# New keys appended to the page tiles of a decode attention, feature chunk innermost

## The chip, the cores and the metric

The kernel runs on one core of a Trainium2 chip. The metric is the device time of one execution in microseconds (us). TensorE (PE) multiplies matrices and writes to the accumulation banks (PSUM), VectorE (DVE), ScalarE (ACT) and GpSimd (POOL) work element by element, and SyncE (SP) issues most DMAs. Each engine works through its own instructions in order and waits on semaphores for the others.

## The reference

Two layers of a causal decoder, run on 256 prompt tokens and on 8 sample batches of 4 new tokens each. Four mixers (pooling, a 31-tap convolution module "conv", a short convolution, and a sparse attention) are gated and summed, and a SwiGLU follows. The change lies in the attention of the sample tokens. Each batch has 256 cached keys, in two pages of 128 rows that a page table names, and 4 new ones:

```
ki_all = concat([cache_kidx[row_ids], ki])            # indexer keys, cached then new
sc = index_scores(qi, ki_all, wi)                     # relu(q.k) weighted over 4 index heads
sc = where(arange(past + t) <= qpos, sc, -inf)        # a new token sees itself and earlier ones
vals, idx = top_k(sc, 65)
kg, vg = keys and values at idx                       # from the pages or from the new tokens
logits = einsum('nqhd,nqkhd->nqhk', q, kg) / 8
out = einsum('nqhk,nqkhd->nqhd', softmax(logits), vg) # 8 heads of 64 features
```

## The kernel before

All 288 tokens (256 prompt, 32 sample) lie along the free axis, features on the partitions. Weights come in 512 KB groups of eight 128x128 tiles. Each is split into a rounded part (`whi`, ACT, L245) and a remainder (`wlo`, DVE, L252) in float32r (fp32r), a format that PE takes in one pass; a float32 (fp32) matmul is split into two instructions. Every weight tile is used in three fp32r matmuls of 288 columns (L271 to L273; L293 to L297 where several outputs are interleaved).

**What sets the order.** The program is written out by a small planner. Weights are drawn by `W`; at each new group of eight tiles (24 matmuls) it counts one tick and calls `side`, which lets the side tasks go on: `index_prompt`, `index_sample`, `attn_prompt`, `attn_sample`, `sconv`, `pool`, and `conv` at low rank. A task is a generator: `yield n` makes it sleep n ticks, `yield d, a` charges the tick's budget of DVE and ACT time. The instructions that it issues stand in the engines' orders at that place. `finish` runs a task to its end. In `layer`, the projections come first, then gates (L1015) and branches (L1030) in turn; the attention and then conv tasks are finished before their branches. After the attention branch, layer 0 has 24 matmuls more (`pe_proj`) than layer 1; then the conv branch starts, interleaved with the first half of `w_o`.

**The conv task's end** in DVE and ACT order: centring (L677), squares (L680), a PE sum (L684), root (L686, ACT with a table load), reciprocal (L691), scaling (L696, L699), sigmoid (L702), product (L706), and in `parts` the rounded half (L633, ACT) and the remainder (L637, DVE), which the conv branch's matmuls take. `pe_load` splits another input there (L303 ACT, L304 DVE).

**The sample attention** runs in two halves `f` of four batches. A page tile `kv` (four buffers) holds both pages of one batch. Keys lie as `[128 features, page, chunk c of 4, 128 keys]`, so that one chunk of a page is 128 neighbouring values. One bank `a` of 128 rows (batch, head, token) takes the scores:
- L946: the bias of unselected keys, brought to the rows by a 0/1 matrix `selh`, in fp32;
- L949: for each chunk, all 32 new keys against all rows, into 32 columns behind the 256;
- L953: for each chunk and batch, that batch's page tile against its 32 rows (four column groups of the array, one per batch).

The bias masks the new keys of other batches too. Then DVE takes the row maximum (L958), ACT the exponential (L964), PE transposes the result (L972, L973), ACT copies it (L975, L976), PE multiplies with the values (L981 new, L984 pages). DVE scales by the reciprocal sum and blanks the other heads' columns (L988), four fp32 matmuls with a 0/1 matrix `sel16` gather the rows (L997), and ACT and DVE write rounded part and remainder (L1002, L1005) for the attention branch. In `index_sample` the cached indexer keys (L902) and the new ones (L904) are multiplied apart, into two banks.

Of the kernel before, what the change touches and what calls it, by code (L numbers as in the profile page):

```python
# [37 lines left out]
BIG = -1.0e30  # L38
# [12 lines left out]
def constants():  # L51
# [15 lines left out]
    ok = (b_[:, None] == b_[None, :]) & (t_[None, :] <= t_[:, None])  # L67
    vb = np.zeros((128, NS))
    vb[:NS] = np.where(ok, 0.0, NEG)
# [11 lines left out]
    c["selh"] = sh.reshape(128, 256)  # L81
    c["hmask"] = (h[:, None] == (np.arange(H))[None, :]) * 1.0
    c["sel16"] = ((j * TS + t)[:, None] == np.arange(16)[None, :]) * 1.0
# [10 lines left out]
    return [np.concatenate(p, 1).astype(np.float32) for p in parts], off  # L94


CONST, COFF = constants()
# [14 lines left out]
class Builder:  # L112
# [749 lines left out]
    def load_kidx(self):  # L862
        nc, l, d = self.nc, self.l, self.d
        self.kx = self.sb.tile([128, 4, 2, 128], F32, name="kv", tag="kv", bufs=4)
        rows = slice(PHYS * l, PHYS * (l + 1))
        for b in range(NB):
            for g in range(2):
                i = 2 * b + g
                if i not in self.page:
                    self.page[i] = nc.sync.value_load(self.pt[0:1, i:i + 1], min_val=0, max_val=PHYS - 1)  # L870
                nc.sync.dma_start(self.kx[64 * (b % 2):64 * (b % 2) + 64, b // 2, g],
                                  d["kidx"][rows][ds(self.page[2 * b + g], 1)].rearrange("a p k -> p (a k)"))
                yield 0, 0.01
            yield 1

    def load_pages(self, which, f):
        nc, l, d = self.nc, self.l, self.d
        rows = slice(PHYS * l, PHYS * (l + 1))
        out = []
        for b in range(4 * f, 4 * f + 4):  # L880
            t = self.sb.tile([128, 2, 4, 128], F32, name="kv", tag="kv", bufs=4)
            for g in range(2):
                nc.sync.dma_start(t[:, g].rearrange("p c k -> p (c k)"),
                                  d[which][rows][ds(self.page[2 * b + g], 1)].rearrange("a p k -> p (a k)"))
            out.append(t)
        yield 1
        return out

    def index_sample(self):
# [4 lines left out]
        for r in range(2):  # L894
            for h in range(4):
                nc.scalar.activation(self.qibd[64 * r:64 * r + 64, :, r, h],
                                     qv[64 * (h % 2):64 * (h % 2) + 64, h // 2, :, r], AF.Copy)
                yield 0, 0.22
        yield 1
        a, a2 = yield from self.get_ax(2)  # L900
        for p in range(4):
            nc.tensor.matmul(a[32 * p:32 * p + 32, :TP], self.qibd[:, p].rearrange("p r h t -> p (r h t)"),  # L902
                             self.kx[:, p].rearrange("p g k -> p (g k)"), start=True, stop=True)
        nc.tensor.matmul(a2[:, :NS], self.qibd.rearrange("p g r h t -> p (g r h t)"), self.ki[:, TP:],  # L904
                         start=True, stop=True)
        nc.tensor.matmul(a2[:, 64:64 + NS], self.c("hsel")[:4], self.wi[:, TP:], start=True, stop=True)
        rl = self.sb.tile([128, N], F32, name="rls", tag="rls", bufs=1)
        nc.scalar.activation(rl[:, :TP], a[:, :TP], AF.Relu, scale=0.0625)
        nc.scalar.activation(rl[:, TP:], a2[:, :NS], AF.Relu, scale=0.0625)
        yield 0, 0.6  # L910
        ws = self.sb.tile([128, NS], F32, name="ws", tag="ws", bufs=1)
        nc.vector.tensor_tensor(ws, a2[:, 64:64 + NS], self.c("delta"), op=OP.mult)
        self.free_ax(2)
# [3 lines left out]
        nc.tensor.matmul(a[:NS, :N], ws, rl, start=True, stop=True)  # L917
        sc = self.sb.tile([NS, N], F32, name="scs", tag="scs", bufs=1)
        nc.scalar.activation(sc[:, :TP], a[:NS, :TP], AF.Copy)
        nc.vector.tensor_tensor(sc[:, TP:], a[:NS, TP:N], self.c("vb")[:NS], op=OP.add)  # L920
        self.free_ax()
        yield 0.2, 0.3
        yield from self.topk(sc, NS, N, TOP_S)
        nc.vector.tensor_scalar(sc, sc, MARK, BIG, op0=OP.not_equal, op1=OP.mult)
        yield 0.3, 0
        self.sbias = sc

    def attn_sample(self):
# [12 lines left out]
        for f in range(2):  # L941
            if f:
                kt = yield from self.load_pages("ck", f)
                yield 1
            a = yield from self.get_ax()
            nc.tensor.matmul(a[:, :N], self.c("selh")[:NS, 128 * f:128 * (f + 1)], self.sbias,  # L946
                             start=True, stop=False)
            for c in range(4):
                nc.tensor.matmul(a[:, TP:N], self.qbd[:, c, 4 * f:4 * f + 4].rearrange("p b h t -> p (b h t)"),  # L949
                                 self.k[:, c, TP:], start=False, stop=False)  # L950
            for c in range(4):
                for j in range(4):
                    nc.tensor.matmul(a[32 * j:32 * j + 32, :TP],  # L953
# [4 lines left out]
            nc.vector.tensor_reduce(st[:, 0:1], a[:, :N], axis=AX.X, op=OP.max)  # L958
# [4 lines left out]
            p = self.sb.tile([128, N], F32, name="rls", tag="rls", bufs=1)  # L963
            nc.scalar.activation(p, a[:, :N], AF.Exp, scale=0.125, bias=st[:, 0:1], accum_out=st[:, 1:2])  # L964
# [8 lines left out]
            nc.tensor.transpose(a[:NS, 256:384], p[:, TP:], ident)  # L973
# [8 lines left out]
            for kc in range(2):  # L982
                for j in range(4):
                    nc.tensor.matmul(a[32 * j:32 * j + 32], pt[:, kc, 32 * j:32 * j + 32],  # L984
                                     vc[j][:, kc].rearrange("p c k -> p (c k)"),
                                     start=False, stop=kc == 1)
# [6 lines left out]
            yield 0.65, 0  # L993
# [7 lines left out]
            v = a[:, :64].rearrange("p (c t) -> p c t", c=4)  # L1001
            nc.scalar.activation(dp[0][:, :, w], v, AF.Copy)  # L1002
            yield 0, 0.25
            yield 1
            nc.vector.tensor_tensor(dp[1][:, :, w], v, dp[0][:, :, w].bitcast(F32), op=OP.subtract)  # L1005
            self.free_ax()
            yield 0.15, 0
# [192 lines left out]
    def run(self):  # L1200
# [56 lines left out]
class Pair:  # L1257
# [9 lines left out]
    "x": (128, KD, N), "w": (NGROUPS, 128, G * 128), "const0": CONST[0].shape, "const1": CONST[1].shape, "par": (L, 128, NPAR),  # L1267
# [35 lines left out]
def lay_out(inp, keys):  # L1303
# [9 lines left out]
    a["const0"], a["const1"] = CONST  # L1313
    par = np.zeros((L, 128, NPAR), f)
# [13 lines left out]
    for g in range(4):  # L1328
# [4 lines left out]
        inp["cache_k"].reshape(L * PHYS, PG, 4, 128).transpose(0, 3, 2, 1)).reshape(L * PHYS, 128, 512)  # L1333
# [40 lines left out]
```

## Time and profile before

| | us |
|---|---|
| median of three timed runs (lowest, highest) | 1090.82 (1090.24, 1092.0) |
| profiled execution, its own time | 1090.84 |
| its span, first to last instruction | 1089.1 |
| PE, DVE, ACT, POOL busy | 1066.8, 770.1, 560.7, 171.6 |

PE is busy nearly all the time, so its instructions set the time together with the few places at which it waits. A matmul's row in the timeline is longer than the step to the next one, since matmuls are pipelined: what one costs is read from start to start. Most of the sum is the 7344 weight matmuls; the sample attention is small beside them.

### The profile page before, as it was taken

The page shows a single profiled execution, that of the slowest core. Times are in us where ns is not written, and L with a number is a line of the kernel's source. Part 1 is how long each engine was busy: PE and PEld are TensorE (multiplying, and loading weights), DVE is VectorE, ACT ScalarE, POOL GpSimd, SP SyncE. Part 2 cuts the span into 40 slices and gives each one's busy share as a digit, 9 for nine tenths or more (in the row PEclk, how much of TensorE's full clock was granted, in tenths as well). Part 3 has the DMA queues.
Part 4 walks back from the last instruction along what each step waited for, and adds up shares of the span by engine and source line. Part 5 has one row for each costly group of instructions (what it writes and reads, how often), then busy time and mean ns, then how long its engine had stood idle before and what let it go on. Part 6 is the DMA issues. An engine that isn't in the chain of part 4 may idle for free.

```text
span 1089.1 us, 20628 instructions
## 1 busy us (share of the span) xinstructions
PE 1066.8 (98%) x8138; PEld 1030.1 (95%) x8138; DVE 770.1 (71%) x1302; ACT 560.7 (51%) x930; POOL 171.6 (16%) x175
## 2 busy tenths in 40 slices
PE   8999999999999999999999999999989999999996
PEld 7999989899999999999999999998989999999995
DVE  5896958579885565544789877776697856655456
ACT  4875445445564444433579564644535644444334
POOL 0730002004510000000527100030045000000004
PEclk9999999999999999999999999999989999999998
DMA  8576556644445455555445854565433654554541
GB/s 302 164 244 212 173 174 232 195 147 135 155 148 184 155 173 168 166 170 167 154 154 171 295 171 155 195 213 184 140 132 117 193 174 156 167 170 166 175 136 44
DMA packets 61299, 188.57 MB, mean 173 GB/s; under 512 B 7538, under 2 KB 11666, under 8 KB 61202
## 3 DMA queue, kind: packets, MB, share of 16 engines
q1 hardware_dynamic: 60210, 183.69, 51.7%
q0 software_dynamic: 992, 3.57, 0.9%
q8 instruction: 64, 1.05, 0.4%
q14 instruction: 33, 0.27, 0.1%
HBM read 182.48 MB, written 4.75 MB: 172 GB/s over the span
## 4 chain that ended last, share of the span: by engine, by line
PE 89%; DVE 5%; issue 2%; ACT 2%; POOL 2%; DMA 1%; SPq 0%; DVEq 0%; POOLq 0%
PE mm L271 24%; PE mm L272 24%; PE mm L273 23%; PE mm L295 2%; PE mm L297 2%; PE mm L293 2%; DVE wlo L252 2%; PE ax L272 1%; PE ax L273 1%; PE ax L271 1%; POOL b L317 1%; PE ax L295 1%; PE ax L297 1%; POOL b L348 1%; PE ax L953 1%
## 5 line engine op out<-in xcount | busy, mean ns | idle before, releaser
L252 DVE TENSOR_TENSOR wlo<-wraw,whi 128x1024 fp32r<-128x1024 f32 (+1 forms) x307 | 383.3, 1251 | 155.0 <-issue 83.8
L271 PE MATMUL mm<-xh,whi 128*128 128x288 f32 x1536 | 455.1, 296 | 0.0
L273 PE MATMUL mm<-xh,wlo 128*128 128x288 f32 x1536 | 453.1, 295 | 0.3 <-DVE wlo L252 0.3
L272 PE MATMUL mm<-xl,whi 128*128 128x288 f32 x1536 | 453.2, 295 | 0.0
L245 ACT ACTIVATE whi<-wraw 128x1024 fp32r<-128x1024 f32 (+1 forms) x307 | 322.6, 1052 | 148.1 <-PE mm L272 74.0
L271 PEld LDWEIGHTS mm<-xh,whi 128*128 128x128 f32 x1536 | 288.8, 188 | 8.1 <-issue 6.4
L273 PEld LDWEIGHTS mm<-xh,wlo 128*128 128x128 f32 x1536 | 288.6, 188 | 0.9 <-DVE wlo L252 0.9
L272 PEld LDWEIGHTS mm<-xl,whi 128*128 128x128 f32 x1536 | 288.8, 188 | 0.3
L271 PE MATMUL mm<-b,whi 128*128 128x288 f32 x576 | 171.0, 297 | 0.3 <-DVE s L1030 0.2
L272 PE MATMUL mm<-b,whi 128*128 128x288 f32 x576 | 169.9, 295 | 0.0
L273 PE MATMUL mm<-b,wlo 128*128 128x288 f32 x576 | 169.7, 295 | 0.0
L271 PEld LDWEIGHTS mm<-b,whi 128*128 128x128 f32 x576 | 108.3, 188 | 1.3 <-issue 0.4
L272 PEld LDWEIGHTS mm<-b,whi 128*128 128x128 f32 x576 | 108.3, 188 | 0.3
L273 PEld LDWEIGHTS mm<-b,wlo 128*128 128x128 f32 x576 | 108.2, 188 | 0.0
L1031 POOL TENSOR_TENSOR m<-m,s 128x288 f32<-128x288 f32 x32 | 35.3, 1129 | 274.6 <-DVE s L1030 274.6
L315 POOL TENSOR_TENSOR b<-xf 128x288 f32<-128x288 f32 x4 | 4.9, 1218 | 442.4 <-DVE xf L1176 433.5
L1149 ACT ACTIVATE b<-s 128x288 fp32r<-128x288 f32 x44 | 19.3, 446 | 92.4 <-DVE s L1144 92.4
L655 DVE SCALAR_TENSOR_TENSOR b<-b,prm 128x256 f32<-128x256 f32 x120 | 62.1, 569 | 0.0
L1144 DVE TENSOR_TENSOR s<-s,mm 128x288 f32<-128x288 f32 x40 | 18.0, 454 | 50.5 <-PE mm L273 50.5
L1015 ACT ACTIVATE g<-mm 128x288 f32<-128x288 f32 x32 | 13.2, 412 | 67.7 <-PE mm L273 67.7
L1015 ACT ACTIVATE xf<-mm 128x288 f32<-128x288 f32 x32 | 13.2, 411 | 51.1 <-PE mm L273 51.0
L1152 DVE TENSOR_TENSOR b<-s,b 128x288 fp32r<-128x288 f32 x44 | 19.8, 458 | 19.5 <-ACT b L1149 19.5
(254 smaller groups left out, 1243.7 us busy)
## 6 DMA issues: line engine op xcount, KB each, us to landing
wraw<-in_w_dram SPq DMA_DIRECT2D x305, 512.0 KB, 3.5
kv<-in_ck_dram SPq DMA_DIRECT2D x32, 256.0 KB, 5.0
kv<-in_cv_dram SPq DMA_DIRECT2D x32, 256.0 KB, 4.3
out_ko_dram<-b POOLq DMA_DIRECT2D x2, 576.0 KB, 4.7
out_vo_dram<-b POOLq DMA_DIRECT2D x2, 576.0 KB, 6.9
kv<-in_kidx_dram SPq DMA_DIRECT2D x32, 32.0 KB, 3.0
xf<-in_x_dram SPq DMA_DIRECT2D x3, 288.0 KB, 6.5
b<-in_p_dram SPq DMA_DIRECT2D x3, 288.0 KB, 4.0
```

Source lines behind the costliest of these rows:

```text
L245: nc.scalar.activation(t[:, c], self.raw[self.nhi][:, c], AF.Copy)
L252: nc.vector.tensor_tensor(t[:, c], raw[:, c], self.hi[self.nlo][:, c].bitcast(F32), op=OP.subtract)
L271: m(out, wh, rh, start=first, stop=False)
L272: m(out, wh, rl, start=False, stop=False)
L273: m(out, wl, rh, start=False, stop=last)
L293: m(o, wh, rh[:, k], start=k == 0, stop=False)
L295: m(o, wl, rh[:, k], start=False, stop=False)
L297: m(o, wh, rl[:, k], start=False, stop=k == nk - 1)
L655: nc.vector.scalar_tensor_tensor(o, e, wj, o, op0=OP.mult, op1=OP.add)
L1015: self.nc.scalar.activation(g, a, AF.Sigmoid)
L1031: nc.gpsimd.tensor_tensor(self.m[:, j], self.m[:, j], t, op=OP.add)
L1152: nc.vector.tensor_tensor(h[:, 1, i % 2], t, h[:, 0, i % 2].bitcast(F32), op=OP.subtract)
```

## The change

New keys become the last four columns of their batch's page tile. For that, the cached keys are laid out on the host with the four feature chunks innermost, a tile is `[128, 260 keys, 4]`, and ACT copies the new keys in (`add_new`). A chunk of a tile is then 260 values, each four values (16 bytes) behind the last. The scores have 260 columns in place of 288, the index scores too (there ACT copies the new indexer keys into the index tile, which stays contiguous). The bias constant becomes a power of two, the bias is written as fp32r, and `selh` is loaded apart and rounded once by POOL, so that L946's successor is one fp32r matmul. The probabilities of new keys are spread over the batches by a mask (`pn`, `own`). ACT, not DVE, scales the output; four transposes take the place of the `sel16` matmuls, and the heads' own rows are picked from them in two pieces.

```diff
-BIG = -1.0e30
+BIG = -(2.0 ** 100)
+NK = TP + TS
...
-        self.kx = self.sb.tile([128, 4, 2, 128], F32, name="kv", tag="kv", bufs=4)
+        self.kx = self.sb.tile([128, 4, NK], F32, name="kv", tag="kv", bufs=4)
...
-            t = self.sb.tile([128, 2, 4, 128], F32, name="kv", tag="kv", bufs=4)
+            t = self.sb.tile([128, NK, 4] if which == "ck" else [128, 2 * PG, 4], F32, name="kv", tag="kv", bufs=4)
...
+    def add_new(self, kt, f):
+        for b, t in enumerate(kt, 4 * f):
+            self.nc.scalar.activation(t[:, TP:].rearrange("p k c -> p c k"),
+                                      self.k[:, :, TP + TS * b:TP + TS * (b + 1)], AF.Copy)
+            yield 0, 0.22
+        yield 1
...
+        for r in range(2):
+            nc.scalar.activation(self.kx[64 * r:64 * r + 64, :, TP:], kn[64 * r:64 * r + 64, :, r], AF.Copy)
+            yield 0, 0.22
         yield 1
-        a, a2 = yield from self.get_ax(2)
+        a = yield from self.get_ax()
...
-        nc.tensor.matmul(a2[:, :NS], self.qibd.rearrange("p g r h t -> p (g r h t)"), self.ki[:, TP:],
-                         start=True, stop=True)
...
-        nc.vector.tensor_scalar(sc, sc, MARK, BIG, op0=OP.not_equal, op1=OP.mult)
+        sbias = self.sb.tile([NS, NK], F32R, name="wi", tag="wi", bufs=1)
+        nc.vector.tensor_scalar(sbias, sc, MARK, BIG, op0=OP.not_equal, op1=OP.mult)
...
                 kt = yield from self.load_pages("ck", f)
-                yield 1
+                yield 2
+            yield from self.add_new(kt, f)
             a = yield from self.get_ax()
-            nc.tensor.matmul(a[:, :N], self.c("selh")[:NS, 128 * f:128 * (f + 1)], self.sbias,
-                             start=True, stop=False)
-            for c in range(4):
-                nc.tensor.matmul(a[:, TP:N], self.qbd[:, c, 4 * f:4 * f + 4].rearrange("p b h t -> p (b h t)"),
-                                 self.k[:, c, TP:], start=False, stop=False)
+            nc.tensor.matmul(a[:, :NK], self.selh[:, 128 * f:128 * (f + 1)], self.sbias, start=True, stop=False)
             for c in range(4):
                 for j in range(4):
-                    nc.tensor.matmul(a[32 * j:32 * j + 32, :TP],
+                    nc.tensor.matmul(a[32 * j:32 * j + 32, :NK],
                                      self.qbd[:, c, 4 * f + j].rearrange("p h t -> p (h t)"),
                                      kt[j][:, :, c], start=False, stop=c == 3)
...
+            pn = self.sb.tile([128, NB, TS], F32, name="pn", tag="pn", bufs=1)
+            nc.vector.tensor_tensor(pn, p[:, None, TP:].to_broadcast([128, NB, TS]),
+                                    self.c("own")[:, NB * f:NB * (f + 1), None].to_broadcast([128, NB, TS]), op=OP.mult)
             nc.vector.reciprocal(st[:, 2:3], st[:, 1:2])
-            yield 0.1, 0
+            yield 0.2, 0
+            yield 1
             a = yield from self.get_ax()
...
-            nc.vector.scalar_tensor_tensor(m.rearrange("p (h d) -> p h d", h=H),
-                                           a.rearrange("p (h d) -> p h d", h=H), st[:, 2:3],
-                                           self.c("hmask")[:, :, None].to_broadcast([128, H, DH]),
-                                           op0=OP.mult, op1=OP.mult)
+            nc.scalar.activation(m, a, AF.Copy, scale=st[:, 2:3])
...
-                nc.tensor.matmul(a[:, 16 * c:16 * c + 16], m[:, 128 * c:128 * (c + 1)], self.c("sel16"),
-                                 start=True, stop=True)
+                nc.tensor.transpose(a[:, 128 * c:128 * (c + 1)], m[:, 128 * c:128 * (c + 1)], ident)
...
+            for e, hi, lo in own:
+                nc.scalar.activation(hi, e, AF.Copy)
+                yield 0, 0.22
+            yield 1
+            for e, hi, lo in own:
+                nc.vector.tensor_tensor(lo, e, hi.bitcast(F32), op=OP.subtract)
+                yield 0.15, 0
...
+        self.selh = self.cst.tile([NS, 256], F32R, name="selh")
+        t = self.s()
+        nc.sync.dma_start(t[:NS, :256], d["selh"])
+        nc.gpsimd.tensor_copy(self.selh, t[:NS, :256])
```

In the rows of the changed kernel the line numbers differ: L955 is the bias matmul, L958 the page matmuls, L1041 the branch product (L1030 before), and the lines of weights, conv and `parts` stand one lower (L270, L690, L695, L698, L705, L636 for L271, L691, L696, L699, L706, L637).

PE in layer 0, from the end of a weight group through the scores of the first half; `scs` or `wi` is the bias, `kv` the page tiles. Before:

```order
L272 MATMUL mm<-xl,whi 128x288
L273 MATMUL mm<-xh,wlo 128x288
L838 MATMUL ax<-const_207,b 128x128 x4
L946 MATMUL ax<-scs,const_207 128x288
L949 MATMUL ax<-b,qbd 128x32 x4
L953 MATMUL ax<-kv,qbd 32x256 x16
L615 MATMUL ax<-b,prm 128x288 x2
```

And in the changed kernel:

```order
L271 MATMUL mm<-xl,whi 128x288
L272 MATMUL mm<-xh,wlo 128x288
L849 MATMUL ax<-b 64x128 x8
L955 MATMUL ax<-wi,selh 128x260
L958 MATMUL ax<-kv,qbd 32x260 x16
L270 MATMUL mm<-xh,whi 128x288
```

The new-key matmuls are gone, and the scores stand one weight group (24 matmuls) later than before.

DVE in layer 1, from the reciprocal's successors to the conv task's last instruction. Before:

```order
L1030 TENSOR_TENSOR s<-mm,g 128x288 x2
L252 TENSOR_TENSOR wlo<-wraw,whi 128x1024
L696 TENSOR_TENSOR b<-b,s 128x288 x2
L699 TENSOR_SCALAR b<-b,prm 128x288
L1030 TENSOR_TENSOR s<-mm,g 128x288 x2
L252 TENSOR_TENSOR wlo<-wraw,whi 128x1024
L699 TENSOR_SCALAR b<-b,prm 128x288
L1030 TENSOR_TENSOR s<-mm,g 128x288 x2
L252 TENSOR_TENSOR wlo<-wraw,whi 128x1024
L706 TENSOR_TENSOR b<-b,s 128x288 x2
L1030 TENSOR_TENSOR s<-mm,g 128x288 x2
L637 TENSOR_TENSOR b<-b 128x288 x2
```

And in the changed kernel, from the reciprocal to the third pair of branch products:

```order
L690 RECIPROCAL s<-s 128x288
L251 TENSOR_TENSOR wlo<-wraw,whi 128x1024
L695 TENSOR_TENSOR b<-b,s 128x288 x2
L698 TENSOR_SCALAR b<-b,prm 128x288 x2
L303 TENSOR_TENSOR b<-b 128x576
L251 TENSOR_TENSOR wlo<-wraw,whi 128x1024
L705 TENSOR_TENSOR b<-b,s 128x288 x2
L1041 TENSOR_TENSOR s<-mm,g 128x288 x2
L251 TENSOR_TENSOR wlo<-wraw,whi 128x1024
L636 TENSOR_TENSOR b<-b 128x288 x2
L1041 TENSOR_TENSOR s<-mm,g 128x288 x2
L251 TENSOR_TENSOR wlo<-wraw,whi 128x1024
```

The conv task's pieces stand earlier against the branch products: all four pairs (L1030, L1041) came after the reciprocal in either kernel, and now only the first of them comes before the remainder (L637, L636).

DVE in layer 0, from the reciprocal to the remainder. Before:

```order
L691 RECIPROCAL s<-s 128x288
L1030 TENSOR_TENSOR s<-mm,g 128x288 x2
L252 TENSOR_TENSOR wlo<-wraw,whi 128x1024
L696 TENSOR_TENSOR b<-b,s 128x288 x2
L699 TENSOR_SCALAR b<-b,prm 128x288
L1030 TENSOR_TENSOR s<-mm,g 128x288 x2
L252 TENSOR_TENSOR wlo<-wraw,whi 128x1024
L699 TENSOR_SCALAR b<-b,prm 128x288
L1030 TENSOR_TENSOR s<-mm,g 128x288 x2
L706 TENSOR_TENSOR b<-b,s 128x288 x2
L637 TENSOR_TENSOR b<-b 128x288 x2
```

And in the changed kernel:

```order
L690 RECIPROCAL s<-s 128x288
L1041 TENSOR_TENSOR s<-mm,g 128x288 x2
L251 TENSOR_TENSOR wlo<-wraw,whi 128x1024
L695 TENSOR_TENSOR b<-b,s 128x288 x2
L698 TENSOR_SCALAR b<-b,prm 128x288
L1041 TENSOR_TENSOR s<-mm,g 128x288 x2
L251 TENSOR_TENSOR wlo<-wraw,whi 128x1024
L698 TENSOR_SCALAR b<-b,prm 128x288
L1041 TENSOR_TENSOR s<-mm,g 128x288 x2
L251 TENSOR_TENSOR wlo<-wraw,whi 128x1024
L705 TENSOR_TENSOR b<-b,s 128x288 x2
L1041 TENSOR_TENSOR s<-mm,g 128x288 x2
```

The remainder (L636) is the next row there. A weight remainder (L251) and the last pair of products have come between, and the rows are those of layer 1 before.

## Rows read from the trace of the kernel before

**Rows 1.** Page, part 1: busy us, share of the span, instructions of each engine.
```profile
PE 1066.8 (98%) x8138; PEld 1030.1 (95%) x8138; DVE 770.1 (71%) x1302; ACT 560.7 (51%) x930; POOL 171.6 (16%) x175
```

**Rows 2.** Waits of PE: who for whom, us in total, times, longest.
```profile
PE ax L271 <- ACT b L633: 3.1, 1, 3.1
PE ax L272 <- DVE b L637: 1.3, 2, 0.8
```

**Rows 3.** Chain of waits, sample attention of layer 0: start us, us, engine, tile, line.
```profile
134.23 0.68 PE ax L946 x2
134.91 1.01 PE ax L949 x8
135.92 1.86 PE ax L953 x32
...
202.37 0.87 PE ax L838 x8
...
218.98 0.80 PE ax L997 x8
```

**Rows 4.** Timeline of PE, first weight matmuls after fp32 work: start us, us, instruction.
```profile
138.57 0.51 PE L271 MATMUL mm<-xh,whi 128*128 128x288 f32 x1
138.92 0.30 PE L272 MATMUL mm<-xl,whi 128*128 128x288 f32 x1
```

**Rows 5.** Timeline of PE, index matmuls of layer 0.
```profile
80.18 0.41 PE L904 MATMUL ax<-ki,qibd 128*128 128x32 f32 x2
80.52 0.40 PE L906 MATMUL ax<-wi,const 4*128 4x32 f32 x2
```

**Rows 6.** Timeline of PE, conv branch of layer 1; in brackets the idle time before.
```profile
793.55 0.29 PE L273 MATMUL mm<-b,wlo 128*128 128x288 f32 x1
796.96 0.61 PE L271 MATMUL ax<-b,whi 128*128 128x288 f32 x1 [3.12 <-ACT b L633]
798.41 0.61 PE L272 MATMUL ax<-b,whi 128*128 128x288 f32 x1 [0.84 <-DVE b L637]
...
819.60 0.30 PE L271 MATMUL mm<-b,whi 128*128 128x288 f32 x1
...
822.64 0.29 PE L273 MATMUL mm<-b,wlo 128*128 128x288 f32 x1
```

**Rows 7.** Timeline of PE, conv branch of layer 0.
```profile
260.02 0.38 PE L271 MATMUL ax<-b,whi 128*128 128x288 f32 x1
260.88 0.40 PE L272 MATMUL ax<-b,whi 128*128 128x288 f32 x1 [0.48 <-DVE b L637]
...
265.06 0.80 PE L293 MATMUL mm<-b,whi 128*128 128x288 f32 x4 [0.68 <-ACT b L1108]
...
281.07 0.30 PE L271 MATMUL mm<-b,whi 128*128 128x288 f32 x1
```

**Rows 8.** Windows: stretch, length, busy us of each engine, granted clock, DMA share, GB/s.
```profile
796.90:802.80 5.90, 5.00 (x18) 4.46 (x19) 5.50 (x10) 1.73 (x4) 3.04 (x4) 0.50 0.39 139
```

**Rows 9.** Timeline of DVE, end of the conv task in layer 1.
```profile
782.19 0.76 DVE L304 TENSOR_TENSOR b<-b 128x576 fp32r<-128x576 f32 x1 [4.28 <-ACT b L303]
...
784.00 1.95 DVE L691 RECIPROCAL s<-s 128x288 f32<-128x288 f32 x1
...
797.45 1.87 DVE L637 TENSOR_TENSOR b<-b 128x288 fp32r<-128x288 f32 x2
```

**Rows 10.** Timeline of ACT, last gate of layer 1.
```profile
781.17 0.41 ACT L1015 ACTIVATE g<-mm 128x288 f32<-128x288 f32 x1
```

**Rows 11.** One line: copies of the queries, ns min/median/max, first and last start us.
```profile
L934 ACT ACTIVATE qbd<-b x16: 213/227/230, 77.1 to 633.7; 64x32 f32<-64x32 f32 x16
```

**Rows 12.** Timelines of SP and POOL at the start.
```profile
22.52 0.42 SPq L1241 DMA_DIRECT2D const<-in_const_dram  x1
25.06 8.90 SPq L239 DMA_DIRECT2D wraw<-in_w_dram  x2
...
29.09 0.80 POOL L519 DMA_DIRECT2D out_convo_dram<-b  x1 [27.17 <-DVE b L517]
```

More of the change, by code (lines that the diff above doesn't have):

```diff
@@ L66, in constants @@
     b_, t_ = bt // TS, bt % TS
-    ok = (b_[:, None] == b_[None, :]) & (t_[None, :] <= t_[:, None])
-    vb = np.zeros((128, NS))
-    vb[:NS] = np.where(ok, 0.0, NEG)
+    vb = np.zeros((128, TS))
+    vb[:NS] = np.where(np.arange(TS)[None, :] <= t_[:, None], 0.0, NEG)
     c["vb"] = vb
@@ L80, in constants @@
         sh[:NS, f] = bt[:, None] == ((4 * f + j) * TS + t)[None, :]
-    c["selh"] = sh.reshape(128, 256)
-    c["hmask"] = (h[:, None] == (np.arange(H))[None, :]) * 1.0
-    c["sel16"] = ((j * TS + t)[:, None] == np.arange(16)[None, :]) * 1.0
+    selh = sh.reshape(128, 256)[:NS].astype(np.float32)
+    c["own"] = np.concatenate([((4 * f + j)[:, None] == np.arange(NB)[None, :]) * 1.0 for f in range(2)], 1)
     win = np.array([2, 4, 8, 16])
@@ L93, in constants @@
         parts[i].append(a)
-    return [np.concatenate(p, 1).astype(np.float32) for p in parts], off
-CONST, COFF = constants()
+    return [np.concatenate(p, 1).astype(np.float32) for p in parts], off, selh
+CONST, COFF, SELH = constants()
 PAR = {"pool_scale": (0, 2), "conv_b": (2, 2), "cg": (4, 2), "cb": (6, 2), "g1": (8, 8), "b1": (16, 8),
@@ L898, in index_sample @@
                 yield 0, 0.22
+        kn = self.ki[:, TP:].rearrange("p (g r t) -> p g r t", g=4, r=2)
+        for r in range(2):
+            nc.scalar.activation(self.kx[64 * r:64 * r + 64, :, TP:], kn[64 * r:64 * r + 64, :, r], AF.Copy)
+            yield 0, 0.22
         yield 1
[L900 removed]
+        a = yield from self.get_ax()
         for p in range(4):
[L902 to L910 removed]
+            nc.tensor.matmul(a[32 * p:32 * p + 32, :NK], self.qibd[:, p].rearrange("p r h t -> p (r h t)"),
+                             self.kx[:, p], start=True, stop=True)
+        nc.tensor.matmul(a[:, 288:288 + NS], self.c("hsel")[:4], self.wi[:, TP:], start=True, stop=True)
+        rl = self.sb.tile([128, NK], F32, name="rls", tag="rls", bufs=1)
+        nc.scalar.activation(rl, a[:, :NK], AF.Relu, scale=0.0625)
+        yield 0, 0.4
         ws = self.sb.tile([128, NS], F32, name="ws", tag="ws", bufs=1)
[L912 to L913 removed]
+        nc.vector.tensor_tensor(ws, a[:, 288:288 + NS], self.c("delta"), op=OP.mult)
+        self.free_ax()
         yield 0.1, 0
@@ L916, in index_sample @@
         a = yield from self.get_ax()
-        nc.tensor.matmul(a[:NS, :N], ws, rl, start=True, stop=True)
-        sc = self.sb.tile([NS, N], F32, name="scs", tag="scs", bufs=1)
+        nc.tensor.matmul(a[:NS, :NK], ws, rl, start=True, stop=True)
+        sc = self.sb.tile([NS, NK], F32, name="scs", tag="scs", bufs=1)
         nc.scalar.activation(sc[:, :TP], a[:NS, :TP], AF.Copy)
-        nc.vector.tensor_tensor(sc[:, TP:], a[:NS, TP:N], self.c("vb")[:NS], op=OP.add)
+        nc.vector.tensor_tensor(sc[:, TP:], a[:NS, TP:NK], self.c("vb")[:NS], op=OP.add)
         self.free_ax()
         yield 0.2, 0.3
-        yield from self.topk(sc, NS, N, TOP_S)
-        nc.vector.tensor_scalar(sc, sc, MARK, BIG, op0=OP.not_equal, op1=OP.mult)
+        yield from self.topk(sc, NS, NK, TOP_S)
+        sbias = self.sb.tile([NS, NK], F32R, name="wi", tag="wi", bufs=1)
+        nc.vector.tensor_scalar(sbias, sc, MARK, BIG, op0=OP.not_equal, op1=OP.mult)
         yield 0.3, 0
-        self.sbias = sc
+        self.sbias = sbias
     def attn_sample(self):
@@ L962, in attn_sample @@
             vc = yield from self.load_pages("cv", f)
-            p = self.sb.tile([128, N], F32, name="rls", tag="rls", bufs=1)
-            nc.scalar.activation(p, a[:, :N], AF.Exp, scale=0.125, bias=st[:, 0:1], accum_out=st[:, 1:2])
+            p = self.sb.tile([128, NK], F32, name="rls", tag="rls", bufs=1)
+            nc.scalar.activation(p, a[:, :NK], AF.Exp, scale=0.125, bias=st[:, 0:1], accum_out=st[:, 1:2])
             self.free_ax()
@@ L1266 @@
 INS = {
[L1267 removed]
+    "x": (128, KD, N), "w": (NGROUPS, 128, G * 128), "const0": CONST[0].shape, "const1": CONST[1].shape, "selh": SELH.shape, "par": (L, 128, NPAR),
     "ck": (L * PHYS, 128, 512), "cv": (L * PHYS, 128, 512), "kidx": (L * PHYS, 64, 128), "p": (L, 128, 2, N),
@@ L1313, in lay_out @@
     a["const0"], a["const1"] = CONST
+    a["selh"] = SELH
     par = np.zeros((L, 128, NPAR), f)
```

26 lines of the change are left out of this document (13 added, 13 removed).

## The prediction

> **What bounds the kernel now.** I read the page's busy shares first, then what PE waited for, then the chain of waits in order of time, and last the timelines of PE, DVE and ACT around two places. PE is busy 98% of the span [rows 1], so an edit counts by the PE time it takes out or puts in, or by a PE wait it makes or ends. The profiled execution took 1090.84 us, 1.74 us more than its span of 1089.1 us; the median of the three timed runs is 1090.82 us, so the sum below is made on 1090.84 and needs no correction. Waits on PE are few: the largest is 3.1 us for the rounded half of the conv result (L633), the next 1.3 us for its remainder (L637) [rows 2]. Both stand where the last branch, conv, begins. Elsewhere PE goes from one matmul to the next every 0.132 us: 23 steps lie between 819.60 and 822.64 [rows 6].
>
> **PE time, per call.** The sample attention runs four times (two layers, two halves). The chain of waits gives the time that each piece holds PE [rows 3]:
> - The four matmuls of all new keys (L949, eight instructions) go: 1.01 us each time, 4.04 us.
> - The bias matmul (L946) takes 0.68 us as fp32. As fp32r it is one pass of 260 columns. An ordinary fp32r matmul takes 0.13 us; the first after fp32 work takes 138.92 - 138.57 = 0.35 us [rows 4], since PE changes over there. The new one stands between fp32 pieces, and the changeover may be paid by it or not at all. I take the middle, 0.24 us: 0.44 us saved, 1.76 us in four (ends 1.3 and 2.2).
> - The select matmuls (L997, eight instructions) take 0.80 us. The four transposes in their place are like L838's, of which eight take 0.87 us, so 0.44 us for four: 0.36 us saved, 1.44 us in four.
> - The index matmul of the new keys (L904) goes: from 80.18 to 80.52, 0.34 us [rows 5], twice: 0.68 us.
> - The page matmuls (L953) get four more columns of 256: 1.86 x 4/256 = 0.03 us, 0.12 us in four. The index matmuls grow by the same share of less, and the score matmul shrinks from 288 to 260 columns; these two I leave out.
>
> 4.04 + 1.76 + 1.44 + 0.68 - 0.12 = 7.8 us less PE work.
>
> **The one price that no row shows** is the reading of the page tile. Before, a page matmul reads 256 neighbouring values; now it reads 260 values, each 16 bytes from the last. No TensorE instruction in this trace streams its moving operand with such a step. A gain is excluded: the instructions are the same in number, with four columns more. The nearest row is L953 itself, 32 instructions in 1.86 us or 58 ns each, with four column groups of the array running side by side. The low end is no change; the high end is that the four run one after the other, 1.86 x 3 = 5.6 us more per call, 22.5 us in all. I take the low end as likeliest. L953 is fp32: eight L838 transposes of 128 columns take 109 ns each, half the column rate of the fp32r stream (288 columns in 132 ns), so each value has about twice the time of an fp32r value to arrive.
>
> **What the order does at the conv branch.** The planner hands ticks to its tasks, and the conv task is low in rank. The added ticks of the sample task move it, and the conv task is let in earlier: in layer 1 its last pieces (L706, L637) now stand three pairs of branch products (L1030) ahead of the branch's end, where one pair followed L706 and none L637 before. So I cost the stretch from the first conv matmul to the last w_o part, 144 matmuls or 19.04 us at 0.132 us.
> - Layer 1 before: PE is ready at 793.68 (a step after 793.55) and has the 144 behind it at 819.60: 25.92 us, 6.9 us lost [rows 6]. It waits 3.1 us, then runs at a granted clock of 0.50, the 1.2 GHz level, from 796.9 to 802.8 [rows 8]. DVE is never idle from 782.19 to that point. Before that it had been idle 4.28 us, since the split L304 stands ahead of the reciprocal L691 and waits for ACT's L303 after the last gate [rows 9].
> - Layer 1 after: L691 stands ahead of that split, three pairs of branch products (72 matmuls, 9.5 us of PE) stand behind L637, and the wait goes. Late next is the first w_o part, which waits for DVE's and ACT's work on its first operand: 0.68 us in layer 0 [rows 7]. I keep 0.7 us.
> - Layer 0 before: 260.02 to 281.07 is 21.05 us, so 2.0 us lost, 0.7 of it at L637 (260.88 in place of 260.15) and 0.68 at the w_o part [rows 7].
> - Layer 0 after: DVE's order becomes that of layer 1 before, piece by piece. There the last gate was done when ACT took it at 781.17 [rows 10], and L637 ended at 799.3, in halves of 0.94 us, while PE was ready at 793.68. In layer 0, 24 more matmuls (pe_proj) stand ahead of the conv branch, so PE is ready 24 x 0.132 = 3.17 us later, at 796.85 on the same scale. L633 is in time. The two L637 halves come at 798.4 and 799.3, the second 1.9 us after PE wants it at 797.4. So 2.0 us lost where 0.7 was: 1.3 us more, 3.3 us in all.
>
> (2.0 + 6.9) - (3.3 + 0.7) = 4.9 us gained. The ends: 2.6 us, if the clock falls in layer 0 too (layer 1's 6.9 less the 3.28 us to 796.96 and the 1.32 us to 798.41 leaves 2.3 us for that); 6.0 us, if layer 0 loses no more than before and layer 1 nothing.
>
> **What is hidden.** The 16 copies of new keys into page tiles and four into the index tile are small ACT work, like L934 at 0.227 us [rows 11]: 20 x 0.227 = 4.5 us of ACT, idle 49% of the span [rows 1]. Four scalings of 128x512 move from DVE to ACT. If that cover failed, PE would wait for a copy at the page matmul; the planner puts a tick, 24 matmuls or 3.2 us, between the copy and its reader, so a wait needs ACT 3 us behind. ACT now waits in order for the page matmuls' sum, and behind it stand a gate's sigmoid and a weight rounding (L245), which run three groups ahead. At the start SP issues one more DMA, for selh, between the constants at 22.52 and weights that do not go before 25.06, and POOL's rounding of it must be over before 29.09, POOL's next work [rows 12]. Nothing is charged for these.
>
> **The sum.** 1090.84 - 7.8 - 4.9 = 1078.1 us.
>
> **Rivals.**
> 1. The spaced reads take twice the time. Then 1.89 us more per call, 7.6 us: 1085.7 us. For it: every value lies 16 bytes on, and four streams are read at once from the same partitions. Against it: the half-rate fp32 pass above.
> The Trainium skill bears on this rival. Its page "SBUF — State Buffer", section "Door 1: The DMA port swizzle", says that reads that go to a new 16-byte line each time pay a penalty and that two hits a line are needed for full rate, but also that a step of four fp32 is free. By its first half this rival is right, by its second the forecast; it gives no factor, and no row here shows such a read.
> 2. The four column groups fall out of step, and the page matmuls run one after the other: 22.5 us more, 1100.6 us, slower. It decides from 12.7 / 4 = 3.2 us more per call, that is at 2.7 times the present 1.86 us. For it: the gain of running side by side is large here, four 256-column instructions in 0.23 us. Against it: each still fills its own quarter of the bank's partitions.
> 3. The conv branch starts no better: the clock falls in layer 0 too, or layer 1's DVE is late in another place, and the 4.9 us shrink to about 0.5. Then 1090.84 - 7.8 - 0.5 = 1082.5 us. For it: DVE has no idle time in these 18 us. Against it: the order itself.
>
> **How the numbers follow.** Forecast 0.47, with 1075.5 to 1080.5 us of its own; rival 1 0.28; rival 3 0.13; rival 2 0.12. About 2 us, 0.2%, is what a measurement here tells from no change, so faster means under 1088.6. The forecast and rival 3 lie there, rival 1 mostly; rivals 1 and 3 together come to 1090, no change, so I say faster 0.76, same 0.11, slower 0.13. A range of 1075.5 to 1089 us leaves out rival 2, the joint case and a little below.
>
> **What would show it.** The page matmuls' group of 32 at 1.9 us per call (forecast), 3.8 us (rival 1) or above 5 us (rival 2). No PE wait for L633 over 1 us in layer 1, and full clock there. About 2 us of waits for the conv remainder in layer 0. Bias matmuls with one instruction each. The forecast is wrong if PE waits newly inside the gates, for the copies, the ACT scaling or the masked new-key weights, since I charged none of these.

## The result and the profile after

| | before | after |
|---|---|---|
| median (lowest, highest), us | 1090.82 (1090.24, 1092.0) | 1084.45 (1083.88, 1085.32) |
| ratio, 95% interval | | 0.9934 [0.9923, 0.9945] |
| profiled execution, us | 1090.84 | 1083.88 |

The changed kernel is 6.4 us faster. The forecast was 1078.1 us. One term more than covers the difference of 6.3 us: the page matmuls cost 7.8 us more than before, where 0.1 us was forecast, which is what rival 1 said of them. The other terms came out close to their working.

In the page's part 1 of the changed kernel (busy us, share of the span, instructions), the line that answers to [rows 1]:

```profile
PE 1063.6 (98%) x8082; PEld 1022.1 (94%) x8082; DVE 767.9 (71%) x1306; ACT 565.2 (52%) x956; POOL 172.6 (16%) x176
```

PE has 56 instructions fewer and is busy 3.2 us less. Its busy share tells nothing of what happened; the waits and the groups do. The waits of PE, changed kernel (us in total, times, longest), for [rows 2]:

```profile
PE mm L270 <- DVE s L1041: 1.8, 1, 1.8
PE mm L292 <- ACT whi L244: 1.3, 2, 1.0
PE ax L1220 <- DVE s L1217: 1.2, 1, 1.2
PE mm L292 <- ACT b L1119: 1.1, 2, 0.7
```

The two waits for the conv result are gone, in both layers. A wait that was not there is now the largest: a weight matmul waits for a branch product (L1041), that is for its bank. The page matmuls, in the chain of waits of the changed kernel (start us, us, engine, tile, line; the count in the chain misses a few of the 32):

```profile
139.22 3.85 PE ax L958 x28
...
198.06 3.81 PE ax L958 x29
```

Each call takes 3.8 us, where L953 took 1.86 [rows 3]. The same call and the transposes in the timeline of PE, changed kernel, for [rows 3, 4]:

```profile
138.84 0.38 PE L955 MATMUL ax<-wi,selh 32*128 32x260 f32 x1
139.15 3.92 PE L958 MATMUL ax<-kv,qbd 128*32 128x260 f32 x32
...
143.00 0.40 PE L270 MATMUL mm<-xh,whi 128*128 128x288 f32 x1
...
174.47 0.60 PE L1002 MATMUL ax<-const,b 128*128 128x128 f32 x4
174.82 0.38 PE L270 MATMUL mm<-b,whi 128*128 128x288 f32 x1
```

From start to start, the bias is one instruction of 0.31 us, the 32 page matmuls take 3.85 us and the four transposes 0.35 us. The conv branch of layer 0 in the same view, for [rows 7]:

```profile
257.14 0.29 PE L272 MATMUL mm<-b,wlo 128*128 128x288 f32 x1
259.24 0.40 PE L270 MATMUL mm<-b,whi 128*128 128x288 f32 x1 [1.81 <-DVE s L1041]
...
260.93 0.29 PE L270 MATMUL ax<-b,whi 128*128 128x288 f32 x1
...
265.02 0.80 PE L292 MATMUL mm<-b,whi 128*128 128x288 f32 x4 [0.67 <-ACT b L1119]
...
281.03 0.30 PE L270 MATMUL mm<-b,whi 128*128 128x288 f32 x1
```

Two microseconds are lost ahead of the conv branch (257.27 to 259.24), halfway through the 24 `pe_proj` matmuls, and 1.06 us inside it (20.10 us for 144 matmuls of 19.04). DVE's timeline, changed kernel, shows why the bank was late:

```profile
244.19 0.76 DVE L303 TENSOR_TENSOR b<-b 128x576 fp32r<-128x576 f32 x1 [4.22 <-ACT b L302]
244.87 1.22 DVE L251 TENSOR_TENSOR wlo<-wraw,whi 128x1024 fp32r<-128x1024 f32 x1
246.00 1.95 DVE L690 RECIPROCAL s<-s 128x288 f32<-128x288 f32 x1
...
257.41 1.41 DVE L705 TENSOR_TENSOR b<-b,s 128x288 f32<-128x288 f32 x2
258.74 0.81 DVE L1041 TENSOR_TENSOR s<-mm,g 128x288 f32<-128x288 f32 x2
```

The products at 258.74, which free the bank, stand behind a weight remainder and two conv pieces. The conv branch of layer 1, PE, changed kernel, for [rows 6]:

```profile
792.93 0.29 PE L270 MATMUL ax<-b,whi 128*128 128x288 f32 x1
...
796.73 0.80 PE L292 MATMUL mm<-b,whi 128*128 128x288 f32 x4 [0.47 <-ACT b L1119]
...
812.74 0.30 PE L270 MATMUL mm<-b,whi 128*128 128x288 f32 x1
```

19.81 us, where it was 25.92 from the moment PE was ready. The windows of the two conv branches (length, busy us of PE, PEld, DVE, ACT and POOL, granted clock, DMA share, GB/s), for [rows 8]:

```profile
258.00:281.00 23.00, 21.09 (x156) 20.81 (x157) 21.87 (x40) 12.05 (x21) 8.36 (x11) 1.00 0.50 162
793.00:813.00 20.00, 19.53 (x147) 19.30 (x146) 18.80 (x35) 9.11 (x15) 9.63 (x12) 1.00 0.51 161
```

The clock is 1.00, the 2.4 GHz level, in both, where it was 0.50 for six microseconds of layer 1.

### The profile page after: what moved, and what is told of

The parts are those of the page before. It is cut to its first block, busy times and chain, and to the rows that moved or that the text cites. A ratio compares the mean times of both kernels' runs of the same rounds, so it can differ in the third digit from the quotient of the medians.

```text
span 1082.1 us, 20554 instructions
## 1 busy us (share of the span) xinstructions
PE 1063.6 (98%) x8082; PEld 1022.1 (94%) x8082; DVE 767.9 (71%) x1306; ACT 565.2 (52%) x956; POOL 172.6 (16%) x176
## 4 chain that ended last, share of the span: by engine, by line
PE 88%; DVE 5%; ACT 2%; issue 2%; POOL 2%; DMA 1%; SPq 0%; DVEq 0%; POOLq 0%; ACTq 0%
PE mm L270 24%; PE mm L271 24%; PE mm L272 24%; PE mm L296 2%; PE mm L294 2%; PE mm L292 2%; DVE wlo L251 2%; PE ax L958 1%; DMA wraw<-in_w_dram 1%; POOL b L316 1%; POOL b L347 1%; PE ax L271 1%; PE ax L993 1%; PE ax L272 1%; PE ax L270 1%
## 5 line engine op out<-in xcount | busy, mean ns | idle before, releaser
L251 DVE TENSOR_TENSOR wlo<-wraw,whi 128x1024 fp32r<-128x1024 f32 (+1 forms) x307 | 382.8, 1249 | 155.4 <-issue 90.1
L270 PE MATMUL mm<-xh,whi 128*128 128x288 f32 x1536 | 455.0, 296 | 0.0
L271 PE MATMUL mm<-xl,whi 128*128 128x288 f32 x1536 | 453.1, 295 | 0.0
L270 PEld LDWEIGHTS mm<-xh,whi 128*128 128x128 f32 x1536 | 288.8, 188 | 9.1 <-issue 8.3
L271 PEld LDWEIGHTS mm<-xl,whi 128*128 128x128 f32 x1536 | 288.8, 188 | 0.3
L270 PE MATMUL mm<-b,whi 128*128 128x288 f32 x576 | 171.0, 297 | 1.9 <-DVE s L1041 1.8
L271 PE MATMUL mm<-b,whi 128*128 128x288 f32 x576 | 169.9, 295 | 0.0
L270 PEld LDWEIGHTS mm<-b,whi 128*128 128x128 f32 x576 | 108.3, 188 | 4.5 <-DVE s L1041 2.0
L271 PEld LDWEIGHTS mm<-b,whi 128*128 128x128 f32 x576 | 108.3, 188 | 0.3
```

The costliest lines, as they stand in the source:

```text
L251: nc.vector.tensor_tensor(t[:, c], raw[:, c], self.hi[self.nlo][:, c].bitcast(F32), op=OP.subtract)
L270: m(out, wh, rh, start=first, stop=False)
L271: m(out, wh, rl, start=False, stop=False)
```

## Experiments

Each kernel was timed in several rounds beside the kernel before on the same chip, except where one run is said. The lines of each kernel are its own; the names in the rows stay the same.

**Contiguous chunks.** Edit, on the changed kernel, in its main lines (the host's layout and the write of the new keys follow):

```diff
-t = ...tile([128, NK, 4] ...)          # which == "ck"
+t = ...tile([128, 4, NK] ...)
...
-nc.sync.dma_start(t[:, PG * g:PG * (g + 1)].rearrange("p k c -> p (k c)"), ...)
+nc.sync.dma_start(t[:, :, PG * g:PG * (g + 1)], src.rearrange("a p (c k) -> p (a c) k", c=4))
...
-                                     kt[j][:, :, c], start=False, stop=c == 3)
+                                     kt[j][:, c], start=False, stop=c == 3)
```

> The changed kernel with the four chunks of a key page contiguous again: a tile is [128, 4 chunks, 260], one chunk is 260 neighbouring values, the transfer writes four pieces of 512 B per partition and page, the new keys are copied behind them; everything else as changed. Theory S (the 16-byte step of the moving operand doubles the page matmuls): they go back from 3.85 to 1.9 us per call, and the time from 1084.4 to about 1084.4 - 4 x 1.96 = 1076.6 us. Rival W (the 3.85 us come from something else in the change: the 260 columns, the copies into the tile just before, the fp32r matmul ahead): they stay at 3.85 us and the time at 1084.4 us. If the smaller pieces make the pages late, PE waits at the page matmuls and the time lies between.

Measured: 1077.08 us, ratio to before 0.9872 [0.9857, 0.9887]. The chain of this kernel:

```profile
139.97 1.89 PE ax L962 x32
...
196.86 1.89 PE ax L962 x32
```

1.89 us per call and 7.4 us less in all, with no wait for the pages. Laid beside the changed kernel, the two PE timelines shift against each other at the four page calls, by 1.9 to 2.1 us each, and after the first 10 us nowhere else by as much as 0.3 us (in those 10 us this execution falls 0.7 us behind). Theory S holds.

**The layout alone, on the kernel before.** Edit: the tile is `[128, 2, 128, 4]`, the read `kt[j][:, :, :, c]`, the host's layout as in the change.

> The kernel before with one edit: the host's layout of the key pages and the tile have the chunk innermost, so the page matmuls read 256 values at a step of 16 bytes; no other part of the change. Theory S: the page matmuls go from 1.86 to 3.8 us per call, four times, and the time from 1090.8 to 1098.6 us. Rival W (the cost needs another part of the change): 1090.8 us.

Measured: 1100.21 us, ratio 1.0083 [1.0069, 1.0097], 8.9 us more than the before of its chip (1091.28). Its chain:

```profile
136.35 3.74 PE ax L953 x32
...
193.07 3.73 PE ax L953 x32
```

No other part of the change is needed for the factor two: 4 x 1.88 = 7.5 us of the 8.9 us are these matmuls, and the two profiled executions (1098.33 and 1090.84 us) differ by just these 7.5 us.

**A step of 8 bytes.** Edit, on the changed kernel: the tile is `[128, 2, NK, 2]`, the read `kt[j][:, c // 2, :, c % 2]`; the host's layout, the transfer and the write of the new keys follow.

> The changed kernel with chunks kept in pairs: a tile is [128, 2 pairs, 260 keys, 2 chunks], so a page matmul reads 260 values at a step of 8 bytes, two values used out of each 16 bytes. Theory L (what counts is how many 16-byte pieces the four column groups read: 4 values each when contiguous, 2 here, 1 when changed): between 1.9 and 2.9 us per call, time 1077 to 1080.5 us. Rival N (any step beyond neighbouring values costs the factor two): 3.85 us per call and 1084.4 us.

Measured: 1078.12 us, ratio 0.9877 [0.9862, 0.9892]. Its chain:

```profile
141.33 1.97 PE ax L963 x27
...
671.18 2.00 PE ax L963 x27
```

2.0 us: theory L, at its lower end. With two used values in every 16 bytes the reads cost 5% more than neighbouring ones; with one, 102% more.

**One column group after another.** Edit, once on the changed kernel and once on the one with contiguous chunks (this one a single run):

```diff
-            for c in range(4):
-                for j in range(4):
+            for j in range(4):
+                for c in range(4):
```

> The changed kernel with the two loops of the page matmuls exchanged: the four chunks of one batch (one column group) follow each other, then the next batch, so that the column groups no longer run side by side. Eight fp32 transposes of 128 columns take 0.87 us, so 32 instructions of 260 columns one after another take about 32 x 0.87 / 16 x 260 / 128 = 3.5 us. Theory P (one read path serves all four column groups, and a 16-byte step takes it to its limit; a single stream alone is not slowed): about 3.5 to 3.9 us per call, time 1083 to 1084.6 us, the same as the changed kernel. Rival Q (each spaced stream runs at half rate by itself): about 7 us per call, time 1084.4 + 4 x 3.2 = 1097 us.

> The kernel of the run with contiguous chunks, with the two loops of the page matmuls exchanged as in the run that took 9.27 us per call at the 16-byte step. Theory P (a single spaced stream is not slowed; the 9.27 us are what one column group after another takes): 9.3 us per call here too. Rival Q (each spaced stream is slowed by itself): 3.5 to 4.7 us per call.

Measured: 1107.42 us, ratio 1.0143 [1.0128, 1.0159], at the 16-byte step; 1087.71 us in the single run with contiguous chunks. The chain at the 16-byte step:

```profile
141.57 9.27 PE ax L958 x29
```

And with contiguous chunks:

```profile
139.62 4.59 PE ax L962 x32
```

9.27 and 4.59 us, a factor of 2.02. Theory P fell: the step slows a stream that runs alone, as much as four that run side by side (3.85 and 1.89). The first expectation had the size of Q too low: its 0.87 / 16 counts the eight transposes as sixteen instructions, which is how it came to 3.5 us for a contiguous call. With the eight that [rows 3] has it would have been 7.1 us, and 4.59 us were measured, so the transposes don't price a page matmul either way.

**Order alone, on the kernel before.** Edit: no instruction is changed, only what the planner is told.

```diff
                 kt = yield from self.load_pages("ck", f)
-                yield 1
+                yield 2
+            yield 1
             a = yield from self.get_ax()
...
             yield 0.1, 0
+            yield 1
...
-            yield 0.65, 0
+            yield 0, 0.65
```

> The kernel before with the same instructions, only their order changed by the numbers that the planner is given: one tick more ahead of the scores of each half (two for the second), one more ahead of the transposes, and the scaling (still on DVE) charged to ACT's budget. In the orders, the conv task's reciprocal then stands ahead of the split of the other input (L304) in both layers, and two pairs of branch products stand behind its remainder. Theory O (order alone makes the gain at the conv branch): layer 1 loses about 0.8 us in place of 6.9, layer 0 about 0.8 to 1 in place of 2.0, so 1090.8 - 7.2 = 1083.6 us, with no wait for L633 over 0.5 us and no clock drop. Rival W (the gain at the conv branch in the changed kernel needs the DVE work that it takes away, 0.65 us of scaling per call): no more than 2 us gained, 1089 us.

Measured: 1085.52 us, ratio 0.9942 [0.9927, 0.9958]: 6.1 us less than its before (1091.62), about as much as the whole change gave. Theory O holds in kind; the gain is 1.1 us short. Of the 5.7 us between the two profiled executions, 4.6 lie between the 48th weight matmul ahead of a conv branch and that branch's end, 1.3 in layer 0 and 3.3 in layer 1. DVE of this kernel in layer 1, for [rows 9]:

```profile
776.51 1.95 DVE L691 RECIPROCAL s<-s 128x288 f32<-128x288 f32 x1
779.50 0.76 DVE L304 TENSOR_TENSOR b<-b 128x576 fp32r<-128x576 f32 x1 [1.04 <-ACT b L303]
...
788.76 1.43 DVE L637 TENSOR_TENSOR b<-b 128x288 fp32r<-128x288 f32 x2
```

The remainder is ready at 790.2, when PE begins the branch at 790.98. But DVE still has two pairs of products and two weight remainders to do, and PE waits for that a little later, in the timeline of PE:

```profile
796.48 1.17 PE L293 MATMUL mm<-b,whi 128*128 128x288 f32 x4 [2.16 <-ACT b L1110]
...
814.02 0.30 PE L271 MATMUL mm<-b,whi 128*128 128x288 f32 x1
```

After it the clock falls (0.73 on the mean from 796.40 to 802.80), so 23.04 us pass from 790.98 to 814.02 and 4.0 us are lost in place of 0.8. The window (columns as for [rows 8]):

```profile
796.40:802.80 6.40, 6.32 (x36) 6.32 (x37) 6.12 (x13) 2.84 (x7) 3.29 (x5) 0.73 0.28 88
```

**The split moved, on the kernel before.** Edit: DVE's half of the split (L304) is issued after the sixth product pair.

```diff
-        self.split(self.pr[:, 0], self.pr[:, 1], pin)
+        nc.scalar.activation(h, pin, AF.Copy)      # DVE's half is issued in branch(), at j == 5
```

> The kernel before with one instruction moved: DVE's half of the split of the other input (L304, 0.76 us, which waits for ACT's half behind the last gate) is issued after the sixth pair of branch products of the attention branch. In layer 1 it stood ahead of the reciprocal, whose operand was there at 779.86, 4.1 us before it started at 784.00. Theory I (DVE's idle time ahead of the split is what makes the conv branch late): the conv pieces come 4.1 - 0.76 = 3.3 us earlier in layer 1, the wait for the rounded half goes and the clock stays up, about 2 us for the remainder are left: 6.9 becomes 2.7 us, and layer 0 gains up to 0.8 us, so 1085.8 to 1086.6 us. Rival V (DVE is late by its volume of work, not by this wait): 1089 to 1091 us.

Measured: 1091.83 us, ratio 0.9997 [0.9988, 1.0006]. Theory I, which is the reason that the prediction gave for layer 1's late conv result, gains nothing. DVE of this kernel in layer 1:

```profile
782.71 1.23 DVE L252 TENSOR_TENSOR wlo<-wraw,whi 128x1024 fp32r<-128x1024 f32 x1 [2.91 <-PE mm L273]
783.85 1.95 DVE L691 RECIPROCAL s<-s 128x288 f32<-128x288 f32 x1
```

With the split away, the weight remainder that stood behind it is still ahead of the reciprocal, and it waits for PE until 782.71. PE's own schedule lies 1.5 us later in this execution by then (1.1 us of it from the first weight groups on; layer 0 lost 0.8 us instead of gaining, 0.73 of them in a wait for a product's bank), so the reciprocal at 783.85 comes 1.7 us earlier against it than in the kernel before, not 4.1, and the split takes 1.3 us of DVE again, four pieces ahead of the remainder. The wait for the rounded half is 2.2 us in place of 3.1, the clock falls all the same (0.60 from 797.50 to 806.00), and the stretch of 144 matmuls, from PE ready, is 25.72 us where it was 25.92. The idle time had two causes in a row; taking away the first showed the second.

**One tick less, with contiguous chunks.** Edit: the `yield 1` between the masked weights `pn` and the transposes goes.

> The kernel of the run with contiguous chunks, less one tick: the one between the masked new-key weights and the transposes. In layer 0 the conv task's reciprocal then comes ahead of the split, as in layer 1 of the changed kernel. Theory I: layer 0's wait for a bank (1.8 us, for DVE's products) and most of what its conv branch loses go, layer 1 stays: 1077.1 - 2.1 = 1075 us. Rival P (without the tick PE waits at the transposes for DVE's masked weights, up to 0.5 us in each of four calls): 1077 us.

Measured: 1081.36 us, ratio 0.9905 [0.989, 0.992], 4.3 us slower than with the tick. The waits of PE, this kernel:

```profile
PE ax L985 <- DVE pn L978: 3.3, 3, 1.9
PE mm L292 <- ACT whi L244: 2.7, 2, 2.1
PE mm L270 <- DVE s L1044: 1.8, 2, 1.5
```

Theory I was right on its own place: from the 48th weight matmul before layer 0's conv branch to its end, 26.42 us pass in place of 28.61, 2.2 us less. Rival P came on top, larger than its 0.5 us a call: PE waits up to 1.9 us for `pn`. It is not the whole loss. The moved pieces also make PE wait 1.5 us for a branch product's bank at 180 us, and this execution is 1.4 us behind by 50 us already, after a wait of 2.1 us for a weight rounding, ahead of anything that the tick moves.

**One number of the planner, both ways, with contiguous chunks.** The instructions are the same; the charge in `add_new` is 0.05 or 0.40:

```diff
-            yield 0, 0.22
+            yield 0, 0.05        # the other kernel: 0, 0.4
```

> The kernel of the run with contiguous chunks, with the same instructions; one number that the planner is given is changed, the ACT time charged for a copy of new keys, from 0.22 to 0.05. In layer 0 DVE's order becomes that of the kernel before with only its order changed: the reciprocal ahead of the split and two pairs of branch products behind the remainder. Layer 1's stays. Theory O (the place of the conv pieces in DVE's order sets what is lost at the conv branch): layer 0 loses 1.0 us in place of 3.0, and the time is 1077.1 - 2.0 = 1075.1 us. Rival M (the earlier copies or other pieces that this number moves give a new wait of that size, as the missing tick did): 1077 us or more.

> The same kernel with that charge at 0.40 instead: DVE's order at the conv branch of layer 1 becomes that of the kernel before (split, weight remainder, reciprocal, and no product behind the remainder), layer 0's stays. No instruction is added or left out. Theory O: layer 1 loses 6.9 us again in place of 0.8, with a wait for the rounded half of 3 us and the lower clock after it, so 1077.1 + 6.1 = 1083.2 us. Rival W (the gain at the conv branch came from less work on DVE, 0.65 us per call of scaling, or from the new instructions): under 1079 us.

Measured: 1074.89 us, ratio 0.9846 [0.9831, 0.9861], with 0.05; 1083.60 us, ratio 0.992 [0.9907, 0.9934], with 0.40. PE of the first at layer 0's conv branch:

```profile
254.72 0.40 PE L270 MATMUL mm<-b,whi 128*128 128x288 f32 x1 [0.29 <-DVE s L1045]
...
256.41 0.29 PE L270 MATMUL ax<-b,whi 128*128 128x288 f32 x1
...
259.93 0.80 PE L292 MATMUL mm<-b,whi 128*128 128x288 f32 x4 [0.18 <-ACT b L1123]
...
275.94 0.30 PE L270 MATMUL mm<-b,whi 128*128 128x288 f32 x1
```

19.53 us, 0.5 lost, and a wait of 0.29 us for a bank ahead of it in place of 1.81. With what that wait costs, 1.0 us is lost around the branch, as forecast: from the 48th weight matmul ahead of it to its end 26.42 us pass, where 192 steps of 0.132 us are 25.4. PE of the second at layer 1's:

```profile
790.06 0.40 PE L270 MATMUL ax<-b,whi 128*128 128x288 f32 x1 [3.12 <-ACT b L632]
791.52 0.40 PE L271 MATMUL ax<-b,whi 128*128 128x288 f32 x1 [1.05 <-DVE b L636]
...
812.48 0.30 PE L270 MATMUL mm<-b,whi 128*128 128x288 f32 x1
```

The wait of 3.1 us is back [rows 2, 6], although DVE's work is that of the changed kernel; the granted clock from 790.05 to 795.80 is 0.70. Theory O holds both times, within 0.4 us of the forecast times. The kernel with 0.05 is faster than both that were compared: 9.6 us below the changed one.

## Why the prediction was right or wrong

**PE work: right.** Summed over the calls, from start to start in the two timelines, the new-key matmuls were 4.03 us (forecast 4.04), the bias went from 2.71 to 1.25 us (1.46 saved, forecast 1.76, inside its ends), select and transposes from 3.24 to 1.50 us (1.74 saved, forecast 1.44), the index matmul 0.68 us (0.68). Together 7.9 us, as forecast without the four columns. The bias came out at 0.31 us and not at the middle 0.24, so more of the changeover is paid than I took; the transposes at 0.375 us a call and not 0.44.

**Page matmuls: wrong.** The step that failed is "I take the low end as likeliest", with its argument that a value has "about twice the time of an fp32r value to arrive". The four calls took 15.25 us in place of 7.46: 7.8 us more, rival 1's 7.6. The argument would have let at least a stream alone run unslowed, and the exchanged loops show that it doesn't: with four column groups side by side or one after another, a 16-byte step doubles the time. An 8-byte step, timed side by side only, adds 5%. The premise was off as well. The 109 ns for 128 columns are those of transposes; a contiguous page matmul alone takes 4.59 us / 32 = 143 ns per instruction of 260 columns, 0.55 ns a column against 0.46 ns for fp32r (132 ns for 288), so a value had 1.2 times as long and not twice.
The first half of the rule that stood beside rival 1, in the Trainium skill, "SBUF — State Buffer", section "Door 1: The DMA port swizzle" (two hits in each 16-byte line are needed for full rate), agrees with both: two hits 2.0 us, one hit 3.85. That section's second half, a free step of four fp32, does not: 102% here. The measurement decides.

**Conv branch: right in size, not in its reason.** Layer 1 lost 0.77 us where 0.7 was forecast (19.81 - 19.04), at full clock and without a wait for the rounded half. Layer 0 lost 1.97 + 1.06 = 3.0 us where 3.3 was forecast, but not at the remainder: DVE was as late as worked out, and PE felt it 12 matmuls earlier, at a bank that a product had not yet released. I had moved the remainder and not asked which other instruction stands behind the same delay. The gain is 46.97 - 41.88 = 5.1 us (forecast 4.9). (The upper end stated for it, 6.0 us, does not follow from its words: 2.0 + 6.9 less 2.0 is 6.9 us.)
Two reasons given for it were wrong. Without the split ahead of the reciprocal nothing is gained in the time of the kernel before, since the weight remainder behind it waits too. And the added ticks alone do not let the conv task in earlier in layer 1: in the order that the planner writes out, the kernel before with the ticks only keeps `split, weight remainder, reciprocal` there, and it takes the charge of the scaling, moved from DVE's budget to ACT's, to change it; the charge without the ticks is enough there. The order-only kernel has both; neither was timed by itself.

**The sum.** 7.9 + 5.1 - 7.8 = 5.2 us; the profiled executions differ by 7.0. Of the other 1.8 us, 0.4 lie in the warm-up matmuls at the start and 0.5 in the score matmul (L917, after L924) and three groups of transposes; about 0.9 us, spread over the weight matmuls elsewhere, stay unassigned (the five runs of the changed kernel spread by 1.4 us). That 1084.45 us lies inside the stated range of 1075.5 to 1089 is owed to rival 1, for which the range had been widened; the forecast's own 1075.5 to 1080.5 missed it.

**Hidden work: right.** No PE wait appeared for the copies, the ACT scaling or `pn` in the changed kernel. That the tick before the transposes is what hides `pn` is shown by the kernel without it (3.3 us of waits). Rival 2 is excluded by the exchanged loops, since at the 16-byte step column groups one after another take 9.27 us and the changed kernel's take 3.85. Its price was also too high: contiguous groups one after another cost 4.59 - 1.89 = 2.7 us more per call, not 5.6. Rival 3 is excluded by the conv branch.

## What to carry to other kernels

A layout that makes a copy convenient can put a step into an operand that PE streams: keep the chunk that PE reads contiguous, or at least two used values in each 16 bytes (5% here), and pay with smaller pieces in the transfer, which nobody waited for here. Where a planner sets the order, a change of work also moves other tasks; time the old work in the new order before crediting the work, since here the order alone gave about as much as the whole change. And when an engine idles ahead of a late instruction, look at everything queued in front of it, not only at the instruction that waits now.

## What the runs showed of the hardware

A contiguous fp32 page matmul (two instructions, 260 columns, 32 rows out) takes 4.59 / 16 = 0.29 us when one column group follows itself, and 1.89 / 16 = 0.12 us when four alternate: side by side gains 2.4, not 4. At the 16-byte step it is 0.58 and 0.24 us, so the gain by alternating stays and the loss by the step is the same factor.

After PE's wait of 1.81 us in layer 0 the granted clock stayed at 1.00 in the changed kernel, in the one with contiguous chunks and in the one with the charge at 0.40. After the same wait it fell to 0.50, the 1.2 GHz level, for 3.4 us in the kernel with the 8-byte step and in both kernels with exchanged loops (one profiled execution of each). PE of the 8-byte step and the window behind it:

```profile
257.65 0.45 PE L270 MATMUL mm<-b,whi 128*128 128x288 f32 x1 [1.81 <-DVE s L1046]
257.86:261.27 3.41, 3.41 (x16) 3.41 (x16) 3.41 (x5) 2.30 (x6) 1.60 (x2) 0.50 0.15 61
```

The fall came with 0.5 us more: from the 48th weight matmul ahead of layer 0's conv branch to its end, 29.1 us pass in these three and 28.6 us in the other three. In layer 1, a wait of 2.16 us in the order-only kernel and one of 3.12 us with the charge at 0.40 were followed by a mean clock of 0.73 and 0.70 over some 6 us, and one of 3.12 us in the kernel before by 0.50 for six microseconds [rows 8]. So a wait at the conv branch can cost more than its length, and its length alone did not tell whether it would.
